# Input projection of a hybrid mixer block: three-pass product on 128-token slabs replaced by Strassen's scheme on 2x2x2 blocks, tokens in two halves

## Chip, cores and metric

One core of a Trainium2 chip. The metric is the device time of one execution in microseconds (us); lower is better. The profile is one execution taken by the hardware profiler on that core. Engines: TensorE (PE for its matmuls, PEld for its weight loads), VectorE (DVE), ScalarE (ACT), GpSimd (POOL) and SyncE (SP, here only an issuer of DMAs).

## What is computed

A pre-norm block on 2048 tokens of width 1024, all float32:

```python
u = rms_norm(h, norm_in_g)
proj = einsum('bsd,de->bse', u, w_in)          # 2048 x 1024 times 1024 x 4096
pool_x, pool_z, m_x, m_z = split(proj, 4)      # 1024 columns each
y_pool = pool_mixer(pool_x, pool_w, pool_scale) * silu(pool_z)   # window means, then pool_w
y_m = mlstm_branch(m_x, ...) * silu(m_z)       # conv, headwise q/k/v, two scans over 16 chunks
h = h + einsum('bse,ed->bsd', concatenate([y_pool, y_m]), w_out)
return rms_norm(h, norm_out_g)
```

Float32 products are made of float32r matmuls: each operand is split into a high part and the rest, and high x high, high x low and low x high are added in PSUM.

## The kernel before

The projection is worked in 32 column slabs of 128 columns by 4 token blocks of 512 tokens. `project` (L135) makes one block of one slab: 8 steps over the 1024 inputs, 3 matmuls each, 24 matmuls of 128x128 by 128x512 into one PSUM tile `proj`; 128 blocks give 3072 matmuls. The normalising factor is not in the operand: x is multiplied by the norm's gain and split as it lands (`uh` by ACT on L217, `ul` by DVE on L218), the factor per token (`rnorm`, L226 to L248) is multiplied in when DVE empties the PSUM tile (L204, L408, L543, L550). A weight slab is loaded whole (`wl`, 512 KB), its high part cast by ACT (L91), its rest made by DVE (L94); it serves all four token blocks. The split of x stays in SBUF for the whole projection.

The order of the slabs: the eight mLSTM slabs first (the *m phase*), then four slabs of m_z, sixteen for the pooling branch (two per pooling slab: `ux` and `sz`), then the other four of m_z. In the m phase each block's columns go through a convolution over tokens (DVE, L314 and L316, five operations of 512 columns, then ACT's silu on L318), and `headwise` (L336 to L346): products to q-k and v maps per 128 tokens, copied out of PSUM by ACT as `tokst` (L337), transposed (L344), copied again as `kkTb` (L346), stored; `gacc` (POOL, L339) sums the gates' rows. In the same phase `fold` multiplies pool_w into the pool_x columns of w_in: 32 steps, each of 6 small matmuls (L185) into a PSUM tile `hw` that `headwise` uses too (3 buffers), a copy by ACT to one tile `st` (L188) and a store to the scratch tensor `wp_s` that ACT's own queue issues (L189). `st` has one buffer, so a copy waits until the store before it has landed. The pooling slabs load their weights from `wp_s`.

After the m phase the gates of all tokens are turned into the scan's tables (L420 to L520): a long chain of small DVE operations with a few matmuls (L456 to L517), beside the first m_z slabs. The last m_z slabs are interleaved with the first steps of the backward scan (`next_backward`, L597). Then comes the main loop, the rest of both scans with the output product (L685), which the change does not touch apart from how it is started.

A scheduler lists the instructions of each engine in an order that respects the data and the buffers and goes by its own estimate of times; from `ordered.append(True)` on the matmuls keep the order in which they are written.

## Time and profile before

| | us |
|---|---|
| median of 3 runs | 1522.79 (1521.84 to 1523.7) |
| profiled execution, its own time | 1520.88 |
| span of that execution, first to last instruction | 1519.2 |
| PE busy / DVE busy / ACT busy / POOL busy | 1493.2 / 845.6 / 494.6 / 359.8 |
| mean granted TensorE clock | 0.994 of full |
| DMA moved | 231 MB, 152 GB/s |

The profiled execution lies 1.7 us above its span and 1.9 us below the median. The projection's last matmul (L135) starts at 858.8 us, the rest of the span is the main loop. [...]

### The profile page before, as it was taken

The page shows a single profiled execution, that of the slowest core. Times are in us where ns is not written, and L with a number is a line of the kernel's source. Part 1 is how long each engine was busy: PE and PEld are TensorE (multiplying, and loading weights), DVE is VectorE, ACT ScalarE, POOL GpSimd, SP SyncE. Part 2 cuts the span into 40 slices and gives each one's busy share as a digit, 9 for nine tenths or more (in the row PEclk, how much of TensorE's full clock was granted, in tenths as well). Part 3 has the DMA queues.
Part 4 walks back from the last instruction along what each step waited for, and adds up shares of the span by engine and source line. Part 5 has one row for each costly group of instructions (what it writes and reads, how often), then busy time and mean ns, then how long its engine had stood idle before and what let it go on. Part 6 is the DMA issues. An engine that isn't in the chain of part 4 may idle for free.

```text
span 1519.2 us, 21070 instructions
## 1 busy us (share of the span) xinstructions
PE 1493.2 (98%) x7193; PEld 1259.9 (83%) x7193; DVE 845.6 (56%) x1700; ACT 494.6 (33%) x1144; POOL 359.8 (24%) x549
## 2 busy tenths in 40 slices
PE   8899999999999999999999999999999999999998
PEld 6788888878888888888888878888888888888886
DVE  8896355563133333445433377767777777665553
ACT  6344433343110011011112444444344445433331
POOL 5544333310000210222200123233332323121100
PEclk8999999999999999999999999999999999999999
DMA  6268765552201111111053787877777778765442
GB/s 223 66 201 234 211 181 169 167 164 80 77 14 56 56 44 53 56 56 44 26 159 107 225 245 233 234 228 207 224 223 216 222 211 262 200 194 156 139 135 84
DMA packets 251339, 231.11 MB, mean 152 GB/s; under 512 B 18400, under 2 KB 211168, under 8 KB 250208
## 3 DMA queue, kind: packets, MB, share of 16 engines
q1 hardware_dynamic: 236768, 215.08, 47.9%
q10 hardware_dynamic: 14464, 14.68, 3.0%
q8 instruction: 57, 0.93, 0.3%
q14 instruction: 50, 0.41, 0.1%
HBM read 149.81 MB, written 79.89 MB: 151 GB/s over the span
## 4 chain that ended last, share of the span: by engine, by line
PE 91%; DVE 3%; DMA 3%; ACT 1%; POOL 1%; issue 1%; SPq 0%; DVEq 0%; POOLq 0%; ACTq 0%
PE proj L135 42%; PE po L685 23%; PE upd L597 7%; PE num L817 7%; PE hw L336 4%; PE num L812 4%; PE sT L802 2%; PE hw L185 1%; PE py L869 1%; DVE ul L218 1%; PE hw L344 1%; DVE c L316 1%; DMA kk<-kk_s 1%; DMA xt<-in_xT 1%; DMA wost<-in_w_out 1%
## 5 line engine op out<-in xcount | busy, mean ns | idle before, releaser
L135 PE MATMUL proj<-uh,whi 128*128 128x512 f32 x1024 | 407.7, 398 | 3.7 <-DVE mx L204 2.3
L135 PE MATMUL proj<-ul,whi 128*128 128x512 f32 x1024 | 402.3, 393 | 2.1 <-DVE ul L218 2.1
L135 PE MATMUL proj<-uh,wlo 128*128 128x512 f32 x1024 | 402.5, 393 | 0.0
L135 PEld LDWEIGHTS proj<-uh,whi 128*128 128x128 f32 x1024 | 194.4, 190 | 43.1 <-DVE mx L204 2.4
L135 PEld LDWEIGHTS proj<-ul,whi 128*128 128x128 f32 x1024 | 194.1, 190 | 41.8 <-DVE ul L218 2.4
L135 PEld LDWEIGHTS proj<-uh,wlo 128*128 128x128 f32 x1024 | 193.9, 189 | 41.2
L685 PE MATMUL po<-woh,yh 128*128 128x512 f32 x512 | 217.6, 425 | 0.0
L685 PE MATMUL po<-woh,yl 128*128 128x512 f32 x512 | 201.5, 394 | 0.0
L685 PE MATMUL po<-wol,yh 128*128 128x512 f32 x512 | 201.3, 393 | 0.0
L597 PE MATMUL upd<-v,kw 128*128 128x258 f32 x480 | 124.2, 381 | 3.1 <-ACT hh L833 1.9
L791 POOL TENSOR_TENSOR cw<-cT,gw 128x512 f32<-128x512 f32 (+1 forms) x64 | 79.0, 1234 | 168.5 <-issue 77.9
L685 PEld LDWEIGHTS po<-woh,yl 128*128 128x128 f32 x512 | 96.2, 188 | 22.1
L685 PEld LDWEIGHTS po<-wol,yh 128*128 128x128 f32 x512 | 96.6, 189 | 19.2
L685 PEld LDWEIGHTS po<-woh,yh 128*128 128x128 f32 x512 | 96.4, 188 | 19.1
L91 ACT CAST whi<-wl 128x1024 fp32r<-128x1024 f32 x31 | 32.6, 1052 | 229.0 <-PE proj L135 225.9
L316 DVE SCALAR_TENSOR_TENSOR c<-mx,par_sb,c 128x512 f32<-128x512 f32 x128 | 103.6, 827 | 3.0
L597 PEld LDWEIGHTS upd<-v,kw 128*128 128x128 f32 x480 | 87.3, 190 | 14.9 <-ACT hh L833 2.0
L543 DVE TENSOR_TENSOR ux<-proj,rnorm 128x512 f32<-128x512 f32 x32 | 22.1, 692 | 124.7 <-PE proj L135 124.7
L784 POOL TENSOR_SCALAR_AFFINE_SELECT gw<-gw 128x128 f32<-128x128 f32 x128 | 43.8, 365 | 172.6 <-DMA gw<-g_s 170.5
L875 ACT ACTIVATE yt<-cT,par_sb 128x128 f32<-128x128 f32 x128 | 44.5, 394 | 108.8 <-DMA ym_s<-yt 108.7
L851 POOL TENSOR_TENSOR rstd<-rstd,mhalf 128x1 f32<-128x1 f32 x64 | 35.1, 549 | 174.5 <-DVE rstd L849 99.8
L833 ACT ACTIVATE hh<-num,rn 128x256 f32<-128x256 f32 x64 | 30.1, 471 | 141.9 <-DVE rn L829 133.8
(194 smaller groups left out, 2184.5 us busy)
## 6 DMA issues: line engine op xcount, KB each, us to landing
gw<-g_s SPq DMA_DIRECT2D x128, 128.0 KB, 4.8
v<-v_s SPq DMA_DIRECT2D x124, 129.0 KB, 4.5
kk<-kk_s SPq DMA_DIRECT2D x124, 128.0 KB, 4.0
wl<-in_w_in SPq DMA_DIRECT2D x23, 512.0 KB, 3.8
xt<-in_xT SPq DMA_DIRECT2D x32, 256.0 KB, 4.8
cT_s<-c SPq DMA_DIRECT2D x32, 256.0 KB, 3.7
kk_s<-tokst SPq DMA_DIRECT2D x32, 256.0 KB, 2.5
kkT_s<-kkTb SPq DMA_DIRECT2D x32, 256.0 KB, 4.1
```

Of the source, the lines that this page charges most:

```text
L91: nc.scalar.copy(hi, src)
L135: pe(nc.tensor.matmul(ps, lhsT=l[:, kt, :], rhs=r[:, kt, :], start=(kt == 0 and n == 0), stop=(kt == KT - 1 and n == 2)))
L316: nc.vector.scalar_tensor_tensor(c, in0=mx[:, b * BT + t:(b + 1) * BT + t], scalar=par_sb[:, i, t:t + 1], in1=c, op0=ALU.mult, op1=ALU.add)
L336: nc.tensor.matmul(ps[:, e, :], lhsT=src[:, o:o + P], rhs=rhs, start=True, stop=True)
L597: pe(nc.tensor.matmul(ps[:, m, :E], lhsT=t["kw"][:, ms], rhs=t["v"], start=True, stop=True))
L685: pe(nc.tensor.matmul(ps, lhsT=l[:, kt, :], rhs=r, start=(kt == 0 and e == 0), stop=(kt == 7 and e == 2)))
L784: nc.gpsimd.affine_select(out=a["gw"][:, 0, d, :], in_=a["gw"][:, 0, d, :], compare_op=ALU.is_ge, fill=BIG, base=0, pattern=[[pat, P]], ch ...
L791: eng.tensor_tensor(a["cw"][:, ds], a["cT"][:, None].broadcast_to([P, nd, 2, P]), a["gw"][:, 1, ds, None, :].broadcast_to([P, nd, 2, P]), ...
L812: pe(nc.tensor.matmul(num[:, d, :E], lhsT=a["dd"][:, d, :], rhs=a["kv"]["v"], start=True, stop=d not in a["dirs"]))
L817: pe(nc.tensor.matmul(num[:, d, :E], lhsT=a["cw"][:, d, m, :], rhs=state[:, m, :], start=False, stop=(m == 1)))
L851: nc.gpsimd.tensor_tensor(a["rstd"][:, 0:1], a["rstd"][:, 0:1], mhalf[:, :1], op=ALU.pow)
L875: nc.scalar.activation(a["yt"][:, m, :], a["cT"][:, m, :], AF.Copy, scale=par_sb[:, i, 8:9])
```

## The change

**Halves.** Tokens are worked in two halves of 1024. In each half all 16 *units* are done in the order m0 to m3, z0, p0 to p7, z1 to z3; a unit is two column slabs of 128 (for p: one of `wp_s` and its z) by two token blocks of 512.

**Seven products.** Each unit takes seven products of 4 input steps x 3 matmuls = 12 matmuls (L153), in the order P1, P5, P6, P2, P7, P3, P4, against 96 matmuls for the same outputs before: 2 x 16 x 84 = 2688 matmuls. P1, P5 and P6 are partial sums: ACT copies them out of PSUM (`snap`, L160), the accumulation in the PSUM tile goes on. P2, P7 and P3 are emptied by DVE as PSUM plus such a copy, P4 by ACT or straight by silu. PSUM: `psy` two tiles, `psx` and `psz` one each.

**Operands.** The weight operands of a unit are 7 quarter sets of 128 x 512, 4 of them sums or differences made by POOL (L141), each cast by ACT (L97) and its rest made by DVE (L100); this is done in both halves, so weights are loaded and prepared twice. The x operands (B) are 7 sets per half; they need the normalised x, so x is scaled in place by gain and factor first (16 DVE operations, L219), then 16 differences (8 on DVE, 8 on POOL, L231) and 28 casts (ACT) and 28 rests (DVE) of 512 columns. The sets of P1 and P2 need the first token block alone, the other five need both. Half 1's x is loaded, scaled and prepared during units 13 to 15 of half 0.

**m phase.** Convolution and `headwise` go in chunks of 4 and 3 token groups (half 0) and 3 x 3 (half 1), and the map tables and a halo of x's tail are passed through DRAM (`mv_s`, `mt_s`). All 32 fold steps are asked for one or two per product from the first unit on, with the fold's tiles in single buffers. The gates' tables come after half 1's m phase, in a pool of their own that is closed before the pooling units' pool is opened at the same addresses.

**End.** Units 13 to 15 of half 1 stand in the written order with `next_backward` after each product; in the last one the main loop's first loads are issued as the x operands' pools close (`room`).

```diff
+    def prepare_a(u, k):
+        w1, w2 = raw[u, 0], raw[u, 1]
+        a11, a12, a21, a22 = w1[:, :4], w1[:, 4:], w2[:, :4], w2[:, 4:]
+        if k in ("P5", "P6", "P7", "P3"):
...
+            v = sums[k] = ap.tile([P, 4, P], F32, name="sum", bufs=3)
+            nc.gpsimd.tensor_tensor(v, x, y, op=op_)
...
+        split(v, hi, lo, nc.vector)
+        A[u, k] = (hi, lo)
+
+    def product(u, k, ps, first):
+        (ah, al), (bh, bl) = A.pop((u, k)), B[k]
+        for q in range(4):
+            for n, (l, r) in enumerate(((ah, bh), (ah, bl), (al, bh))):
+                pe(nc.tensor.matmul(ps, lhsT=l[:, q, :], rhs=r[:, q, :], start=(first and q == 0 and n == 0),
+                                    stop=(q == 3 and n == 2), skip_group_check=not first))
...
+    def unit(u, nxt, put, between):
+        for n, k in enumerate(PRODUCTS):
+            if k == "P1":
+                y = banks["y"] = psp.tile([P, BT], F32, name="psy", bufs=2)
+            bank = "x" if k == "P2" else "z" if k in ("P5", "P3") else "y"
+            if k in ("P5", "P2"):
+                banks[bank] = psp.tile([P, BT], F32, name=f"ps{bank}")
+            ps = banks[bank]
+            product(u, k, ps, k in ("P1", "P5", "P2"))
+            if k in ("P1", "P5", "P6"):
+                snap(k, ps)
+            elif k == "P4":
+                put(1, 0, ps, None)
+            else:
+                e, t, other = {"P2": (0, 0, "P1"), "P7": (1, 1, "P5"), "P3": (0, 1, "P6")}[k]
+                put(e, t, ps, snaps[other])
+            if nxt:
+                prepare_a(nxt, k)
+            between(n)
...
+    def scale_x(t, kt):
+        nc.vector.scalar_tensor_tensor(xs[t, kt], in0=xs[t, kt], scalar=par_sb[:, kt, 9:10], in1=rn[t], op0=ALU.mult,
+                                       op1=ALU.mult)
...
+    def prepare_b(k):
+        hi = bpool[k].tile([P, 4, BT], F32R, name=f"bh{k}")
+        lo = bpool[k].tile([P, 4, BT], F32R, name=f"bl{k}")
+        for q in range(4):
+            x11, x12, x21, x22 = xs[0, q], xs[1, q], xs[0, 4 + q], xs[1, 4 + q]
+            v = {"P1": x11, "P5": x11, "P6": x11, "P2": x21, "P7": x12, "P3": x22, "P4": x21}[k]
+            if k in ("P5", "P6", "P7", "P4"):
+                x, y = {"P5": (x12, x11), "P6": (x22, x11), "P7": (x22, x12), "P4": (x21, x11)}[k]
+                (nc.vector if k in ("P5", "P6") else nc.gpsimd).tensor_tensor(v, x, y, op=ALU.subtract)
+            split(v, hi[:, q], lo[:, q], nc.vector)
+        B[k] = (hi, lo)
+
+    plan = [("m", i) for i in range(4)] + [("z", 0)] + [("p", i) for i in range(8)] + [("z", i) for i in range(1, 4)]
...
+    folds = (None for g in range(4) for _ in fold(g))
+    for p in range(2):
...
+        if p == 0:
+            fop = open_pool(pm, "fop", bufs=1)
+        for n in range(5):
+            u = plan[n]
+
+            def between(k, n=n):
+                chunk_step(p)
+                if p == 0:
+                    next(folds, None)
+                    if n:
+                        next(folds, None)
...
+        if p:
+            pmp.close()
+            with ExitStack() as pz:
+                gp = open_pool(pz, "gp")
+                psg = open_pool(pz, "psq", bufs=2, space=PSUM)
+                gate_rows()
+        with ExitStack() as pz:
+            zp = open_pool(pz, "pp", bufs=2)
+            for n in range(5, 13):
+                put, ux, sz = put_p(p, plan[n])
+                unit(plan[n], after(p, n), put, lambda k: None)
...
+                for n in range(13, 16):
+                    unit(plan[n], after(p, n), put_z(p, plan[n]), lambda k, n=n: between(k, n))
```

The order of three places, before and after. ACT in the m phase, among the fold's copies and stores; `c` is the convolution's silu, `mv` and `mw` the map tables, `P_` a copied partial sum, `tokst` and `kkTb` headwise's results. Before:

```order
L188 COPY st<-hw 128x256
L189 DMA wp_s<-st 128x2x128
L188 COPY st<-hw 128x256
L189 DMA wp_s<-st 128x2x128
L188 COPY st<-hw 128x256
L189 DMA wp_s<-st 128x2x128
L318 ACTIVATE c<-c,par_sb 128x512
L305 COPY mw<-pg 128x16
L306 ACTIVATE mw<-pg 128x128
L307 COPY vw<-pg 128x16
L337 COPY tokst<-hw 128x2x144 x4
L346 COPY kkTb<-hw 128x512
```

After:

```order
L269 COPY st<-hw 128x256
L270 DMA wp_s<-st 128x2x128
L269 COPY st<-hw 128x256
L270 DMA wp_s<-st 128x2x128
L321 ACT_TABLE_LOAD
L321 ACTIVATE c<-c,par_sb 128x512
L321 ACTIVATE c<-c,par_sb 128x384
L296 COPY mv<-pg 128x16
L297 ACTIVATE mv<-pg 128x128
L298 COPY mv<-pg 128x16
L160 COPY P_774<-psz 128x512
L269 COPY st<-hw 128x256
```

Before, 32 copies stand in 179 rows of ACT; after, they stand in 155 rows, and 169 projection matmuls stand among the folds' on PE.

PE where the gates' tables end (`decr`, `mpr`, `glr`, `gm`, `wsr` are the tables; `pg` its PSUM tile). Before:

```order
L135 MATMUL proj<-uh_113,wlo 128x512
L499 MATMUL pg<-decr,ones 128x128
L500 MATMUL pg<-ones,mpr 128x1
L501 MATMUL pg<-ones,glr 128x1
L135 MATMUL proj<-uh_113,whi 128x512
L135 MATMUL proj<-ul_114,whi 128x512
L135 MATMUL proj<-uh_113,wlo 128x512
L135 MATMUL proj<-uh_113,whi 128x512
L135 MATMUL proj<-ul_114,whi 128x512
L516 MATMUL pg<-ident,gm 128x128
L135 MATMUL proj<-uh_113,wlo 128x512
L135 MATMUL proj<-uh_113,whi 128x512
```

After:

```order
L153 MATMUL psy<-bhP_4091,alP_6138 128x512
L551 MATMUL pg<-decr,ones 128x128
L552 MATMUL pg<-ones,mpr 128x1
L553 MATMUL pg<-ones,glr 128x1
L568 MATMUL pg<-ident,gm 128x128
L569 MATMUL pg<-ident,wsr 128x128
L153 MATMUL psx<-bhP_4191,ahP_6196 128x512
L153 MATMUL psx<-blP_4192,ahP_6196 128x512
L153 MATMUL psx<-bhP_4191,alP_6197 128x512
L153 MATMUL psy<-bhP_4288,ahP_5879 128x512
```

Before, projection matmuls stand between the first three and each of the last two; after, the five stand in a row, ahead of the next unit's `psx` and of the fourth product of the unit before (`psy`).

DVE at the same place after (`ux` and `sz` are the pooling unit's results):

```order
L560 TENSOR_SCALAR gm<-g_6034,mg 128x128
L570 TENSOR_TENSOR em_tok<-pg,b_tok 128x128
L572 COPY ws_tok<-pg 128x128
L407 TENSOR_TENSOR ux<-psx,P_6135 128x512
L411 TENSOR_TENSOR sz<-psy,P_6154 128x512
L407 TENSOR_TENSOR ux<-psz,P_6174 128x512
```

The three results of the pooling unit, two of which PE's next tiles wait for, stand behind the last row of the gates' chain.

DVE at the start. Before (`ul` is the rest of x's split, `sq` a square's sum, `mx` an emptied PSUM tile):

```order
L218 SCALAR_TENSOR_TENSOR ul_114<-xt,par_sb,uh_113 128x512 x4
L230 TENSOR_TENSOR sq<-sq 128x512
L228 TENSOR_TENSOR sq<-sq 128x512 x2
L230 TENSOR_TENSOR sq<-sq 128x512
L218 SCALAR_TENSOR_TENSOR ul_109<-xt,par_sb,uh_108 128x512
L230 TENSOR_TENSOR sq<-sq 128x512
L218 SCALAR_TENSOR_TENSOR ul_109<-xt,par_sb,uh_108 128x512
L204 TENSOR_TENSOR mx<-proj,rnorm 128x512 x2
L218 SCALAR_TENSOR_TENSOR ul_109<-xt,par_sb,uh_108 128x512 x5
```

After, from the second token block's scaling on (`x_` a block of x, `bl` a rest of an x operand, `bh` its cast):

```order
L219 SCALAR_TENSOR_TENSOR x_182<-x_182,par_sb,rn_314 128x512
L219 SCALAR_TENSOR_TENSOR x_184<-x_184,par_sb,rn_314 128x512
L231 TENSOR_TENSOR x_150<-x_170,x_150 128x512
L231 TENSOR_TENSOR x_152<-x_172,x_152 128x512
L231 TENSOR_TENSOR x_154<-x_174,x_154 128x512
L100 TENSOR_TENSOR blP_325<-x_150,bhP_324 128x512
L100 TENSOR_TENSOR blP_325<-x_152,bhP_324 128x512
L100 TENSOR_TENSOR blP_325<-x_154,bhP_324 128x512
L231 TENSOR_TENSOR x_156<-x_176,x_156 128x512
```

Before, a rest needs the cast of the same block alone; after, a block is scaled by the norm's result, then differences are taken, and the rests come from these.

## Rows read from the trace of the kernel before

**Rows 1.** The page: chain that ended last, shares by engine and line.

```profile
PE 91%; DVE 3%; DMA 3%; ACT 1%; POOL 1%; issue 1%; SPq 0%; DVEq 0%; POOLq 0%; ACTq 0%
PE proj L135 42%; PE po L685 23%; PE upd L597 7%; PE num L817 7%; PE hw L336 4%; PE num L812 4%; PE sT L802 2%; PE hw L185 1%; PE py L869 1%; DVE ul L218 1%; PE hw L344 1%; DVE c L316 1%; DMA kk<-kk_s 1%; DMA xt<-in_xT 1%; DMA wost<-in_w_out 1%
```

**Rows 2.** Windows (us): sum, busy by engine (instructions), clock, DMA share, GB/s.

```profile
0.00:80.00 80.00, 68.88 (x302) 56.69 (x303) 65.26 (x74) 36.32 (x60) 46.52 (x45) 0.89 0.45 145
...
100.00:320.00 220.00, 216.38 (x1325) 193.18 (x1324) 119.38 (x158) 98.75 (x232) 81.15 (x168) 1.00 0.70 196
```

**Rows 3.** Windows of the projection's line alone: sum, PE, PEld busy.

```profile
0.00:80.00 80.00, 57.94 (x210) 44.10 (x211) 0.89 0.45 145
...
100.00:320.00 220.00, 125.27 (x509) 92.93 (x509) 1.00 0.70 196
...
340.00:764.00 424.00, 423.22 (x1865) 349.40 (x1863) 1.00 0.15 53
```

**Rows 4.** Windows of the start, columns as in the second group.

```profile
0.00:20.00 20.00, 15.42 (x58) 12.86 (x59) 13.95 (x14) 13.03 (x19) 9.94 (x17) 0.83 0.82 286
...
40.00:60.00 20.00, 15.16 (x66) 12.28 (x65) 20.00 (x20) 7.92 (x13) 15.04 (x11) 0.90 0.37 107
```

**Rows 5.** Groups by form: line, engine, tiles, count, busy us, mean ns, idle before.

```profile
L218 DVE SCALAR_TENSOR_TENSOR ul<-xt,par_sb,uh 128x512 fp32r<-128x512 f32 x32 | 35.3, 1152 | 0.0
...
L204 DVE TENSOR_TENSOR mx<-proj,rnorm 128x512 f32<-128x512 f32 x32 | 21.7, 687 | 85.9 <-PE proj L135 82.7 <-ACT rnorm L248 3.1
...
L94 DVE TENSOR_TENSOR wol<-wost,woh 128x512 fp32r<-128x512 f32 x9 | 6.1, 690 | 5.5 <-ACT woh L91 3.3 <-DMA sz_s<-op 2.2
...
L217 ACT ACTIVATE uh<-xt,par_sb 128x512 fp32r<-128x512 f32 x32 | 21.0, 711 | 1.3 <-DMA xt<-in_xT 1.3
...
L188 ACT COPY st<-hw 128x256 f32<-128x256 f32 x32 | 11.8, 368 | 37.3 <-DMA wp_s<-st 32.0 <-PE hw L185 3.3 <-PE pg L304 1.7
```

**Rows 6.** Timeline of DVE at the start: start, us, operation, count.

```profile
53.15 5.33 DVE L218 SCALAR_TENSOR_TENSOR ul<-xt,par_sb,uh 128x512 fp32r<-128x512 f32 x4
...
59.60 2.06 DVE L218 SCALAR_TENSOR_TENSOR ul<-xt,par_sb,uh 128x512 fp32r<-128x512 f32 x3
```

**Rows 7.** Timeline of POOL at the start, same columns.

```profile
46.25 1.47 POOL L240 TENSOR_TENSOR rs<-rs,mhalf 128x4 f32<-128x4 f32 x1 [1.36 <-DVE rs L239]
...
52.75 1.37 POOL L226 TENSOR_TENSOR sq<-xt 128x512 f32<-128x512 f32 x1
54.09 1.73 POOL L228 TENSOR_TENSOR sq<-sq 128x512 f32<-128x512 f32 x1
```

**Rows 8.** The fold's tile: copies, what ACT waited for (us, times), landing.

```profile
L188 ACT COPY st<-hw x32: 349/372/387, 87.9 to 311.9; 128x256 f32<-128x256 f32 x32
...
  DMA wp_s<-st: 32.0, 9
...
DMA to landing us min/median/max: 1.8/3.2/4.9
```

**Rows 9.** Timeline of ACT at three fold copies in a row.

```profile
226.19 0.37 ACT L188 COPY st<-hw 128x256 f32<-128x256 f32 x1 [4.21 <-DMA wp_s<-st]
...
228.48 0.37 ACT L188 COPY st<-hw 128x256 f32<-128x256 f32 x1 [1.92 <-DMA wp_s<-st]
```

**Rows 10.** Timeline of DVE along the gates' chain.

```profile
323.61 0.23 DVE L424 COPY fx<-gacc 128x128 f32<-128x128 f32 x1 [2.48 <-POOL gacc L339]
...
350.66 0.29 DVE L502 COPY dec_bc<-pg 128x128 f32<-128x128 f32 x1 [0.67 <-PE pg L501]
...
355.23 0.28 DVE L520 COPY ws_tok<-pg 128x128 f32<-128x128 f32 x1
```

**Rows 11.** Timelines of two weight rests, alone and beside POOL.

```profile
454.72 1.23 DVE L94 TENSOR_TENSOR wlo<-wl,whi 128x1024 fp32r<-128x1024 f32 x1 [0.17 <-ACT whi L91]
...
476.39 3.62 POOL L556 TENSOR_TENSOR win<-ux 128x2063 f32<-128x2063 f32 x1 [17.92 <-DVE ux L543]
476.52 4.58 DVE L94 TENSOR_TENSOR wlo<-wl,whi 128x1024 fp32r<-128x1024 f32 x1 [0.21 <-ACT whi L91]
```

More of the change, by code (lines that the diff above doesn't have):

```diff
@@ new lines, in product, with snap @@
+    def product(u, k, ps, first):
[4 more added lines that the diff above has]
+                                    stop=(q == 3 and n == 2), skip_group_check=not first))
+    banks, snaps = {}, {}
+    def snap(name, ps):
+        snaps[name] = ap.tile([P, BT], F32, name=name)
+        nc.scalar.copy(snaps[name], ps)
@@ new lines, in hymba_block, with chunk_step, put_mx, put @@
+    CHUNKS = (((0, 4), (4 * P, 3)), tuple((FIRST + 3 * n * P, 3) for n in range(3)))
+    convs, maps = [], []
+    def chunk_step(p):
+        if maps:
+            headwise(p, *maps.pop(0))
+        if convs:
+            maps.append(convs[0])
+            conv(p, *convs.pop(0))
+    def put_mx(p, u):
+        def put(e, t, ps, other):
+            i = 2 * u[1] + e
+            if i not in made:
+                new_mx(p, i)
+                made.add(i)
+            a = at(p, p * S // 2 + t * BT)
+            dst = mxs[i][:, a:a + BT]
+            if other is None:
+                nc.scalar.copy(dst, ps)
+            else:
+                nc.vector.tensor_tensor(dst, ps, other, op=ALU.add)
+            if p == 0 and t == 1:
+                nc.sync.dma_start(out=mt_s[i], in_=mxs[i][:, FIRST:])
+        made = set()
+        return put
@@ L395, in hymba_block @@
-    phw.close()
-    def z_slab(zp, i, order):
-        w = load_w(w_in[24 + i])
-        for b in order:
-            z_block(zp, i, w, b)
-    def z_block(zp, i, w, b, between=None):
-        ps = project(w, b, range(KT // 2))
-        if between:
-            between()
-        project(w, b, range(KT // 2, KT), ps)
-        sz = zp.tile([P, BT], F32, name="op")
-        nc.vector.tensor_tensor(sz, ps, rnorm[:, b * BT:(b + 1) * BT], op=ALU.mult)
-        nc.scalar.activation(sz, sz, AF.Silu)
-        nc.scalar.dma_start(out=sz_s[i][:, b * BT:(b + 1) * BT], in_=sz)
```

573 lines of the change are left out of this document (278 added, 295 removed).

## Prediction

> **What bounds the kernel now.** I read the chain of waits first: TensorE holds 91% of it, and 42% of the span is the projection's line alone [rows 1]. So matmuls taken out of the projection are worth their full time wherever TensorE is never late. The windows tell where that is. From 340 to 764 us it is busy all the time, and the projection's line has 1865 matmuls in 423.2 us [rows 3], 0.227 us each. In the first 80 us it is busy 68.9, and VectorE 65.3 [rows 2]; from 40 to 60 VectorE is never idle and TensorE is at 15.2 of 20 [rows 4]. From 100 to 320 TensorE is busy 216.4 of 220 [rows 2]. So two kinds of stretch: those where fewer matmuls are time gained, and the start and the m phase, where the other engines are close behind. I read next what the change puts on these. The main loop after 859 us is not touched.
>
> **The gain.** 3072 - 2688 = 384 matmuls x 0.227 = **-87 us**. A product is 12 x 0.227 = 2.72 us, a unit 19.05. In the pooling and z units I expect this in full: a unit asks VectorE for 7 weight rests (0.69 each [rows 5]) and 3 evacuations (0.69), 7 us, a pooling unit's windows on 1032 columns for up to four operations at twice 0.69, 6 more, within 19; the copies of partial sums lie two products ahead of their use. These costs I set at nothing; TensorE's work covers them. Elsewhere:
>
> **Start.** Before, TensorE has 210 projection matmuls done by 80 us [rows 3], because a block of x is split as it lands. After, only P1 and P2 can start on the first norm, the rest wait for the second. GpSimd carries the norms: per block 4 squares of 1.37, 2 sums of 1.73 and a power of 1.47 [rows 7], 10.4 us, plus 3 weight sums before the first power; from the first landing at about 6 us that gives the first norm at 6 + 10.4 + 3 x 1.4 + some 5 of waits, about 26. VectorE then scales 8 blocks, makes 8 rests and the square sums (20 operations), and the second norm comes out near 49 (20 x 0.69, 8 of them slowed beside GpSimd by 0.6, and some 4 for the power and its spreading). The price of that neighbour: four rests in a row took 5.33 us beside GpSimd and three took 2.06 alone [rows 6], 1.33 against 0.69. Then 8 scalings, 8 differences and 20 rests stand on VectorE: 36 x 0.69 = 25, and 10 slowed by 0.6 make 31, to 80; the last product ends near 82. By then TensorE has about 99 matmuls of the projection. 111 missing x 0.227 = 25, and 2 us past 80: **+28** (21 to 35, the ends being all pairs alone and all slowed).
>
> **Folds.** This is the largest unknown. The order puts all 32 fold copies into 155 rows of ScalarE, while TensorE's matching rows hold 169 projection matmuls (38.3 us) and 192 fold, 56 headwise (two records each), 28 transposes and 15 map matmuls. In 100 to 320 the small ones cost (216.4 - 509 x 0.227) / (1325 - 509) = 0.124 per record [rows 2, 3], so 347 x 0.124 = 43 and TensorE has 81 us to do there. ScalarE's own operations in those rows sum to 59 us (32 copies at 0.37, 17 casts, 36 headwise copies and so on, by their groups as in [rows 5]). But each copy waits for the store of the copy before it: one buffer, and the store is issued behind it on the same queue. Before, nine such waits took 32.0 us, 3.6 each; the landing is 1.8 to 4.9, median 3.2 [rows 8], and a copy right behind another waited 4.21 and 1.92 [rows 9]. Going through the 155 rows with one landing time for all, ScalarE needs 81 us at 1.9, 98 at 2.5, 104 at 2.7, 116 at 3.1, 129 at 3.55 and 158 at 4.5. Queued behind the waiting copy are the copies of partial sums, the weight casts and headwise's copies, so TensorE waits too. Before, the copies were spread over 225 us and their waits of 32 us hidden. The stores carry the same bytes beside similar traffic, so I take 3.1, next to the median: 115 - 81 = **+33** (0 to 50).
>
> **Half 1's x.** During units 13 to 15 VectorE gets 16 scalings, 8 differences, 28 rests, 14 weight rests and 6 evacuations with the norm's sums: about 76 x 0.7 = 53 us, and some 22 beside GpSimd's differences and sums pay 0.6 each, together 66. It can start when the first norm is there, about 24 us into unit 13 (load of 4 MB at the 286 GB/s of the first 20 us [rows 4], 15 us, and the norm). 24 + 66 + 2.7 = 93, where TensorE would be through with half 1's first unit at 4 x 19.05 = 76: **+17** (8 to 28).
>
> **Gates.** The chain from the summed gates to the table of decays took 323.6 to 350.7, 27 us, and to the last table 355.2 [rows 10]. Before, TensorE had z slabs to do beside it, without end. After, the next pooling unit's results wait, in VectorE's order and for their addresses, behind the chain; the PSUM tiles fill, and the matmuls in TensorE's order ahead of L551 are some 18 us. So 27 - 18 = 9, then 5 from the decays to the last table with nothing between, and about 3 until three evacuations (0.69 each [rows 5]) free PSUM: **+17** (12 to 22). The cover that is gone is the z slabs.
>
> **Rest.** Half 1's m phase: per unit TensorE has 19 and 18 token groups x 5 records x 0.124 = 11, together 30, and VectorE 10 operations of 0.69 and 6 convolutions of five operations on 384 columns (16), together 23: hidden but for single waits, +2 (0 to 8). The start of the main loop, whose first loads are now issued some 5 us later against the last product: +4 (0 to 10). No row shows either; the bounds are one evacuation more or less per product and one landing of 4.9 us [rows 8] twice. What TensorE lost before in 80 to 859 us (about 5 us, of it 3.6 in 100 to 320 [rows 2]) is contained in these terms: -5.
>
> **Sum.** -87 + 28 + 33 + 17 + 17 + 2 + 4 - 5 = +9. The profiled execution was 1520.9, so 1530. It lies 1.9 under the median of the runs, within their spread of 2.
>
> **Rivals.**
>
> *The folds hide.* If the stores land in about 1.9 us the stretch falls to TensorE's 81 and the term to nothing: 1530 - 33 = **1497**, faster than before. For it: the least landing is 1.8, and one of two waits in a row was 1.92 [rows 9]; in half 0 fewer stores of headwise run beside. Against it: nine waits at 3.6 on average. It decides below a landing of about 2.7 us: there the stretch is 104, and the whole sum is near nothing.
>
> [...] One weight rest of 1.23 us took 4.58 when GpSimd's addition of 3.62 began just before it [rows 11], close to the sum of both, 4.85. If every pair at the start and in half 1's preparation paid the plain sum, the 10 and 22 pairs would each pay GpSimd's 1.4 instead of 0.6, +8 and +18: about **1556**. Against it: a pair of short operations took 1.33 + 1.37 side by side, not one after the other [rows 6, 7]. [...]
>
> [...]
>
> *The change doesn't do what it says:* the products could come out slower than 0.227 where `psx` and `psz` have one tile each; an evacuation of 0.69 against a product of 2.72 between speaks against it.
>
> **Chances.** Forecast 0.53 (own range 1512 to 1548), folds hidden 0.25, port 0.14, clock 0.08. Faster and slower by more than 0.2% (3 us) is about what a measurement of this kernel can tell from no change. Faster: folds hidden 0.25 and the forecast's lower end 0.06, 0.31. Within 0.2% of 1522.8: 0.10, from the forecast's middle of small landings. Slower: 0.59. The range runs from folds hidden with the gates at their lower bound, 1494, to the port's 1560; left out are the clock and a tail of the port and of the folds, 0.15.
>
> **What would show it.** The changed kernel's product line has 2688 matmuls; in a pooling unit 84 of them take 19 us. The first unit's last matmul stands near 80 us, with VectorE full from 50. Between 82 and 200 us ScalarE's copies wait for stores, 50 to 60 us in all, and TensorE's idle time there is ended by ScalarE. TensorE waits for VectorE's rests of x operands at the turn of the halves (near 470 to 490), and for the gates' chain once, 15 us or more, ahead of L551. The last matmul of the projection starts near 868. It is wrong if the waits for stores are short and TensorE is full in the fold stretch, or if the preparation of x takes no longer than TensorE's units beside it.

## The result and the profile after

The changed kernel takes 1635.55 us (median of 4 runs, 1634.38 to 1636.11) against 1522.6 for the kernel before in the same comparison: ratio 1.074 (95% interval 1.0722 to 1.0759), 113 us slower. The prediction was 1530, with a range to 1560. The profiled run has a span of 1632.7, 113.5 above the span before.

From the page of the changed kernel come the busy line of TensorE and the others (busy us, share, instructions), the granted clock in 40 slices, and the chain that ended last by engine (to be set against [rows 1]).

```profile
PE 1470.6 (90%) x6809; PEld 1210.9 (74%) x6809; DVE 1021.5 (63%) x1994; ACT 650.4 (40%) x1506; POOL 579.7 (36%) x763
...
PEclk6699999999988999979999989999999999999999
...
PE 58%; DVE 9%; DMA 9%; issue 5%; POOL 4%; ACT 3%; SPq 0%; POOLq 0%; DVEq 0%; ACTq 0%
```

TensorE's share of the last chain fell from 91% to 58%. It is busy 1470.6 us, 22.6 less than before, though 384 matmuls of 0.227 were taken out, 87 us: some 64 us were given back, most of it by matmuls at a lower granted clock (slices 1, 2, 12, 13, 18 and 24 of the clock row, at 0.6 to 0.8 of full, show it best; the mean granted clock is 0.954, against 0.994). The rest of the loss is idle time, 162 us of the span against 26.

Next the windows of the changed kernel, cut at the ends of its units (the 84th, 168th, ... matmul of the product line); columns as in [rows 2].

```profile
0.00:86.80 86.80, 43.74 (x139) 31.31 (x140) 65.57 (x80) 32.38 (x55) 47.27 (x42) 0.63 0.24 79
86.80:275.80 189.00, 160.03 (x857) 128.69 (x856) 86.87 (x122) 80.26 (x202) 86.02 (x150) 0.96 0.62 178
275.80:333.00 57.20, 57.20 (x254) 47.37 (x253) 29.15 (x34) 20.86 (x37) 25.49 (x23) 1.00 0.25 84
333.00:457.00 124.00, 116.01 (x505) 94.09 (x504) 71.62 (x82) 43.29 (x75) 68.88 (x55) 1.00 0.28 96
457.00:516.70 59.70, 48.49 (x201) 39.30 (x199) 51.67 (x60) 26.12 (x47) 31.86 (x22) 0.89 0.27 91
516.70:691.50 174.80, 152.71 (x767) 126.87 (x767) 132.68 (x197) 91.09 (x217) 56.92 (x100) 0.94 0.49 154
691.50:753.50 62.00, 48.47 (x204) 38.68 (x203) 40.99 (x133) 20.22 (x39) 19.84 (x43) 0.86 0.28 91
753.50:875.00 121.50, 115.78 (x505) 94.20 (x504) 70.37 (x82) 41.65 (x72) 63.85 (x51) 1.00 0.23 79
875.00:955.60 80.60, 73.44 (x313) 59.93 (x311) 35.19 (x50) 29.79 (x55) 14.38 (x12) 0.96 0.41 129
955.60:1632.70 677.10, 654.73 (x3077) 550.45 (x3076) 437.35 (x1156) 264.72 (x714) 165.20 (x271) 0.99 0.69 201
```

And the product line alone in three of them, as in [rows 3]:

```profile
0.00:86.80 86.80, 33.78 (x85) 21.64 (x86) 0.63 0.24 79
86.80:275.80 189.00, 95.25 (x337) 61.60 (x336) 0.96 0.62 178
...
516.70:691.50 174.80, 114.85 (x421) 82.31 (x420) 0.94 0.49 154
```

Taking a product matmul at 0.227 and a small record at 0.124 (both worked out from [rows 2, 3]), each stage can be set against the TensorE work that is in it:

| stage (us of the changed kernel) | length | TensorE's work at full clock | loss | predicted |
|---|---|---|---|---|
| start, to the first unit's end (0 to 86.8) | 86.8 | 125 product matmuls fewer than before at 80, and 6.8 later | 35 | 28 |
| half 0, units 1 to 4 with the folds (86.8 to 275.8) | 189.0 | 337 x 0.227 + 520 x 0.124 = 141 | 48 | 33 |
| pooling and z units (275.8 to 457 and 753.5 to 875) | 302.7 | 1264 x 0.227 = 287 | 16 | 0 |
| turn of the halves (457 to 516.7) | 59.7 | 169 x 0.227 and 32 of one column = 40 | 20 | 17 |
| half 1, units 0 to 4 (516.7 to 691.5) | 174.8 | 421 x 0.227 + 346 x 0.124 = 138 | 36 | 2 |
| gates, units 5 and 6 (691.5 to 753.5) | 62.0 | 42 | 20 | 17 |
| last units (875 to 955.6) and the main loop behind them | 80.6 and 677.1 | 70, and 660.2 as before | 10 and 17 | 4 |

The losses sum to 202; less the 87 of the change's gain and the 5 that TensorE lost before, 110 of the 113.5 are found. In the pooling and z units TensorE runs at full clock and a unit takes 19.0 to 20.9 us, so the gain itself is there.

**Where it waits.** Each place is shown by lines of the timelines (start, us, engine, operation, idle time before and what ended it). First a pooling unit, GpSimd, then ScalarE, then TensorE:

```profile
341.60 1.29 POOL L141 TENSOR_TENSOR sum<-w 128x512 f32<-128x512 f32 x1 [2.57 <-DMA w<-in_w_in]
...
344.28 0.62 ACT L97 CAST ahP<-sum 128x512 fp32r<-128x512 f32 x1 [0.74 <-POOL sum L141]
344.80 0.58 ACT L160 COPY P<-psy 128x512 f32<-128x512 f32 x1
...
345.43 0.50 PE L153 MATMUL psy<-bhP,ahP 128*128 128x512 f32 x1 [1.45 <-ACT P L160]
```

The weight load has one buffer per tile and was issued at 337.7, when the unit before had read it. GpSimd's sum waits for it, ScalarE's cast waits for the sums, and behind that cast in ScalarE's queue stands the copy of a partial sum which frees TensorE's tile: 1.45 us here. Eleven of the fifteen pooling and z units of the table take 20.1 to 20.9 us in place of 19.0. Over the whole run such waits for a weight load come to 123.5 us of GpSimd and ScalarE.

Next half 1's m phase, the same three engines:

```profile
590.71 1.27 POOL L141 TENSOR_TENSOR sum<-w 128x512 f32<-128x512 f32 x1 [5.08 <-DMA cT_s<-c]
...
592.02 0.62 ACT L97 CAST ahP<-sum 128x512 fp32r<-128x512 f32 x1 [3.02 <-POOL sum L141]
...
593.02 1.29 ACT L341 COPY tokst<-hw 128x288 f32<-128x288 f32 x4
...
598.80 0.61 ACT L321 ACTIVATE c<-c,par_sb 128x384 f32<-128x384 f32 x1 [3.97 <-DVE c L319]
...
600.31 1.28 ACT L341 COPY tokst<-hw 128x288 f32<-128x288 f32 x4
...
593.48 0.51 PE L340 MATMUL hw<-mv,mx 128*128 128x144 f32 x2 [1.78 <-ACT tokst L341]
...
600.76 0.51 PE L340 MATMUL hw<-mv,mx 128*128 128x144 f32 x2 [2.25 <-ACT tokst L341]
```

At 590.71 GpSimd's sum starts after 5.08 us; its weights were asked for at 586.3, behind five stores in SyncE's queue (the wait is put down to a store that came with it). ScalarE's cast waits for the sum, headwise's copies stand behind the cast, and TensorE waits 1.78 for them; five us later the head of ScalarE's queue is a silu that waits 3.97 for VectorE's convolution, and TensorE waits 2.25 for the copies behind it. That convolution had itself begun late, behind a rest that waited 2.95 us for ScalarE's cast, so the two waits hang together. The windows right there show the clock around such a gap:

```profile
599.00:603.00 4.00, 2.24 (x11) 1.91 (x12) 2.59 (x5) 2.95 (x8) 0.59 (x2) 0.90 0.41 130
603.00:607.00 4.00, 4.00 (x20) 3.51 (x19) 2.11 (x5) 2.00 (x5) 0.27 (x1) 0.68 0.32 116
```

In 603 to 607 TensorE is busy all the time and granted 0.68 of full clock (0.50 from 603 to 605, then 0.70 and 1.00 in a microsecond each): behind the gap it loses time again. The same is seen at the start, where a matmul ahead of a wait of 5.05 us took 0.39 and the one behind it 0.79; from 60 to 80 us the granted clock was 0.50:

```profile
53.71 0.39 PE L153 MATMUL psy<-bhP,alP 128*128 128x512 f32 x1
59.15 0.79 PE L153 MATMUL psz<-bhP,ahP 128*128 128x512 f32 x1 [5.05 <-ACT bhP L97]
```

Not every gap is paid so: the pooling units of 333 to 457 us have 8 us of idle time in gaps like the one above, and a clock of 1.00.

Then the turn of the halves, and the gates, both on TensorE (the last line is from the table of waits between 691.5 and 753.5: us in total, times, longest):

```profile
463.12 1.86 PE L207 MATMUL pg<-ones,sq 128*128 128x1 f32 x8 [4.14 <-DVE sq L203]
...
478.26 1.02 PE L207 MATMUL pg<-ones,sq 128*128 128x1 f32 x8 [3.91 <-DVE sq L203]
```

```profile
709.60 0.66 PE L508 MATMUL pg<-lfr,le 128*128 128x64 f32 x2 [4.70 <-DVE lfr L500]
...
727.90 0.79 PE L551 MATMUL pg<-decr,ones 1*128 1x128 f32 x2 [6.34 <-ACT decr L549]
...
PE psx L153 <- DVE ux L407: 1.2, 1, 1.2
```

In both, small matmuls of a norm or of the gates' chain stand early in TensorE's order and it waits in line for VectorE's sums (8.1 us), the table's transposed rows (4.7) and the decays (6.3). For a pooling unit's result it waited 1.2 us in the gates' two units. Last, the start of the main loop (SyncE, ScalarE, TensorE):

```profile
969.58 0.38 SPq L736 DMA_DIRECT2D y<-yp_s  x1
...
977.54 0.40 ACT L97 CAST yh<-y 128x256 fp32r<-128x256 f32 x1 [11.33 <-DMA y<-yp_s]
...
978.00 0.79 PE L759 MATMUL po<-woh,yh 128*128 128x512 f32 x1 [7.80 <-ACT yh L97]
```

The second y is asked for at 969.6, lands at 977.5, and TensorE stands for 7.8 us.

### The profile page after: what moved, and what is told of

Same layout as the page of the kernel before. It is cut to its first block, busy times and chain, and to the rows that moved or that the text cites. A ratio compares the mean times of both kernels' runs of the same rounds, so it can differ in the third digit from the quotient of the medians.

```text
span 1632.7 us, 21715 instructions
## 1 busy us (share of the span) xinstructions
PE 1470.6 (90%) x6809; PEld 1210.9 (74%) x6809; DVE 1021.5 (63%) x1994; ACT 650.4 (40%) x1506; POOL 579.7 (36%) x763
## 4 chain that ended last, share of the span: by engine, by line
PE 58%; DVE 9%; DMA 9%; issue 5%; POOL 4%; ACT 3%; SPq 0%; POOLq 0%; DVEq 0%; ACTq 0%
PE po L759 20%; PE psy L153 10%; PE upd L672 6%; PE num L891 6%; PE psz L153 5%; PE num L886 3%; PE psx L153 2%; DVE alP L100 2%; POOL win L430 2%; PE hw L340 2%; POOL sum L141 2%; PE sT L876 2%; DVE c L319 1%; DMA w<-in_w_in 1%; DMA wost<-in_w_out 1%
## 5 line engine op out<-in xcount | busy, mean ns | idle before, releaser
L153 PE MATMUL psy<-bhP,ahP 128*128 128x512 f32 x512 | 214.2, 418 | 25.3 <-ACT P L160 18.0
L153 PE MATMUL psy<-blP,ahP 128*128 128x512 f32 x512 | 209.5, 409 | 4.4 <-DVE blP L100 4.4
L153 PE MATMUL psy<-bhP,alP 128*128 128x512 f32 x512 | 207.8, 406 | 0.0
L100 DVE TENSOR_TENSOR alP<-sum,ahP 128x512 fp32r<-128x512 f32 x128 | 122.3, 956 | 104.6 <-ACT ahP L97 94.3
L97 ACT CAST ahP<-sum 128x512 fp32r<-128x512 f32 x128 | 79.2, 620 | 206.3 <-POOL sum L141 96.6
L153 PEld LDWEIGHTS psy<-bhP,ahP 128*128 128x128 f32 x512 | 101.6, 199 | 52.6 <-ACT P L160 24.2
L153 PEld LDWEIGHTS psy<-blP,ahP 128*128 128x128 f32 x512 | 101.3, 198 | 26.2 <-DVE blP L100 6.6
L153 PEld LDWEIGHTS psy<-bhP,alP 128*128 128x128 f32 x512 | 100.9, 197 | 20.7
L319 DVE SCALAR_TENSOR_TENSOR c<-mx,par_sb,c 128x384 f32<-128x384 f32 (+1 forms) x160 | 113.8, 719 | 3.9
L153 PE MATMUL psz<-bhP,ahP 128*128 128x512 f32 x256 | 103.6, 405 | 6.7 <-ACT bhP L97 6.1
L153 PE MATMUL psz<-blP,ahP 128*128 128x512 f32 x256 | 102.0, 398 | 1.7 <-DVE blP L100 1.7
L97 ACT CAST ahP<-w 128x512 fp32r<-128x512 f32 x96 | 59.4, 620 | 110.5 <-PE psy L153 70.2
L153 PE MATMUL psz<-bhP,alP 128*128 128x512 f32 x256 | 101.7, 397 | 0.0
```

Of the source, the lines that this page charges most:

```text
L97: nc.scalar.copy(hi, src)
L100: lo_eng.tensor_tensor(lo, src, hi.bitcast(F32), op=ALU.subtract)
L153: pe(nc.tensor.matmul(ps, lhsT=l[:, q, :], rhs=r[:, q, :], start=(first and q == 0 and n == 0), stop=(q == 3 and n == 2), skip_group_check ...
L319: nc.vector.scalar_tensor_tensor(c[:, :m], in0=mx[:, o + t:o + t + m], scalar=par_sb[:, i, t:t + 1], in1=c[:, :m], op0=ALU.mult, op1=ALU.add)
```

## The experiments

Times are medians; ratios are to the kernel before in the same comparison, with 95% intervals. The changed kernel itself is at 1.074. A difference of 0.003 is 4.6 us. Stages are read from one profiled execution of each kernel, and a stage that an edit doesn't touch differs between kernels too: half 0's units 1 to 4 took 186.6 to 193.3 us in the changed kernel and the five whose edits lie elsewhere, half 1's units 0 to 4 took 173.2 to 176.8 in seven such, and units 5 and 6 of half 1 took 60.4 to 63.6 in eight.

**The store behind the fold's copy.** `a_st3`:

```diff
-            st = fop.tile([P, 2, P], F32, name="st", bufs=1)
+            st = fop.tile([P, 2, P], F32, name="st", bufs=3)
```

> The changed kernel with three buffers in place of one for the fold's copied tile, so that a copy need not wait for the store before it. Theory A (the prediction's fold term: landings of the stores hold ScalarE, and TensorE behind it): the time falls by about 33 us, 1600, and the loss of half 0's m phase (86.8 to 275.8 us, 189 us against 141 us of TensorE work) mostly goes. Theory B (in-order queues: ScalarE's copies out of PSUM stand behind whatever its head waits for, and the store is only one of several such heads; the trace shows 15.2 us of waits for stores and TensorE held 6.9 us by these copies): the time falls by 5 to 12 us, 1624 to 1631.

It takes 1633.27 us, ratio 1.0721 (1.069 to 1.0752): 2 to 3 us less, and the interval holds the changed kernel's 1.074. What ScalarE waited for in front of the copies and their landings, first in the changed kernel, then here:

```profile
  DMA wp_s<-st: 15.2, 11
...
DMA to landing us min/median/max: 1.8/2.4/6.6
```

```profile
  PE hw L266: 32.6, 24
  DMA wp_s<-st: 4.2, 2
```

The prediction's largest cost is not there: 15.2 us of waits in all, landings of 2.4, and when those waits go, the copies wait for the folds' matmuls instead (32.6 us), with TensorE hardly earlier: units 1 to 4 took 186.8 us, within what untouched kernels show. Theory B's 5 to 12 us aren't there either.

**The folds as a whole**, left out of both kernels. `a_nofold` and `b_nofold` (lines of the first's edit):

```diff
-        for e, t in enumerate((wp_s[i], w_in[8 + i]) ...
+        for e, t in enumerate((w_in[i], w_in[8 + i]) ...
...
-                    next(folds, None)
```

> The changed kernel without the folds (the 32 steps that multiply pool_w into the weights are left out; the pooling units take their unfolded weights from the input). TensorE's share of the folds is 192 matmuls x 0.12 = 23 us. Theory A (the folds and their single buffers make half 0's loss): falls by 23 + 40 or more, to 1570 or less. Theory B (headwise's copies behind casts and silus in ScalarE's queue make it, folds or not; half 1, which has no folds, loses 36 us as well): falls by 23 + 10 to 20, 1593 to 1603.

> The kernel before without the folds, left out in the same way; it gives the folds' price there. Both theories: TensorE is busy throughout that phase, so its 23 us of fold matmuls go and little else, 1497 to 1502.

The changed kernel without folds takes 1595.01, 1.047 (1.0439 to 1.05), 41 us less; the kernel before takes 1497.96, 0.9833 (0.9803 to 0.9863), 25.5 less, TensorE's own work of 23 and little more. So the folds cost 15 us more in the changed kernel than before. The four units without folds:

```profile
86.80:237.00 150.20, 126.65 (x665) 107.28 (x664) 84.04 (x122) 69.29 (x169) 36.70 (x70) 0.95 0.58 163
```

They take 150.2 us for 337 x 0.227 + 328 x 0.124 = 117 us of work: two thirds of half 0's loss is there without any fold.

**The fold's split weights.** `a_fop2`: two buffers for `wh` and `wlf` (`bufs=1` to `bufs=2` in the pool).

> The changed kernel with two buffers for the fold's split weights (wh, wlf), as the kernel before has. Leaving the folds out took 40.5 us from the changed kernel and 25.6 from the one before; three buffers for the copied tile took 2. Theory D (the other 13 us are TensorE waiting in line for GpSimd's split of the next weights, 11.4 us in the trace, because one buffer lets it begin only after the fold before): 8 to 13 us less, 1622 to 1627. Rival (the folds cost through ScalarE's and PSUM's queues): under 4 us.

It takes 1629.06, 1.0708 (1.0666 to 1.075), 5 to 6 us less with an interval that holds 1.074. Units 1 to 4 took 186.1 in place of 189.0, next to the lowest of the untouched kernels. The theory's 8 are not shown, nor is a smaller share of the 15 for these buffers or for the store. TensorE's wait for GpSimd's split of these weights, 11.4 us in the changed kernel and none in the kernel before, is still there with two buffers, 11.9; it is the largest wait that comes with the folds, and what holds the split back was not tried.

**Weight loads.** `a_w2`: a second pair of raw weight tiles for every other unit, where SBUF has room:

```diff
-            raw[u, e] = ap.tile([P, KT, P], F32, name=f"w{e}")
+            raw[u, e] = (wide[0] or ap).tile([P, KT, P], F32, name=f"w{e}")
...
+            w2 = open_pool(pz, "w2p")
```

> The changed kernel with a second pair of raw weight tiles, used by every other unit in half 1's m phase and in both halves' pooling units, so that the next load need not wait until the unit before has read its weights. Theory B (a late weight load holds GpSimd's sums, these ScalarE's casts, and behind the casts stand the copies of partial sums that TensorE waits for: 20.5 us per pooling unit in place of 19.0, and gaps in half 1's m phase): every second pooling unit comes to 19.0 us, and half 1's m phase gains some; together 12 to 25 us less, 1611 to 1624. [...]

It takes 1621.8, 1.0625 (1.0583 to 1.0666), 14 to 17 less. Six pooling and z units of half 0 (8 to 13) now:

```profile
338.00:452.00 114.00, 114.00 (x504) 94.41 (x503) 62.46 (x82) 41.82 (x73) 56.95 (x50) 1.00 0.26 86
```

They take 114.0 us in place of 124.0, TensorE busy throughout, 19.0 per unit where they took 20.4 to 20.9, and half 1's units 7 to 12 take 19.0 each as well. The chain from the load to the partial sum's copy is the whole loss of these units. Half 1's m phase gained 4 (170.9 us). These stages gain 21 together; the turn of the halves took 4 longer (63.9), so the whole run shows less.

**The gates.** `a_gate` keeps the tables' pool open beside the pooling units' (both in one `with`); `a_gatesplit` does that and cuts the chain in four parts that are written behind units 4, 5, 7 and 8:

```diff
+        yield
         pr = psg.tile([P, 512], F32, name="pg")
         nc.tensor.matmul(pr[:, :P], lhsT=ones[:1, :], rhs=flat(decr), start=True, stop=True)
...
+                if p and n in (5, 7, 8):
+                    next(gates, None)
```

> The changed kernel with the gates' tables in a pool that stays open beside the first pooling units of half 1, so that their results have addresses of their own and the scheduler may put them between the rows of the gates' chain. The prediction's gate term (results and PSUM behind the chain): 12 to 22 us go, 1613 to 1623, and units 5 and 6 of half 1 take 40 to 45 us together in place of 62. Rival (VectorE's chain itself and its place in the queue hold TensorE, whatever the addresses): under 5 us.

> The changed kernel with the gates' tables in a pool that stays open (as in a_gate, which gained 1 us) and, in addition, the chain written in four parts, behind units 4, 5, 7 and 8 of half 1, so that the chain's matmuls stand later in TensorE's order: 150 product matmuls (34 us) now lie between the table's transposed rows and the decays, where it was 83 rows or fewer. Theory C (addresses don't matter; TensorE's order reaches the chain's matmuls before VectorE has their operands and waits in line): units 5 and 6 of half 1 take 38 to 43 us in place of 62, total 15 to 22 us less, 1613 to 1621. Rival (VectorE's chain takes the results' place in its own queue whatever the matmuls' order): under 6 us.

`a_gate` takes 1634.52, 1.0729 (1.0698 to 1.076), 1 to 2 less, which can't be told from nothing. Units 5 and 6 of half 1:

```profile
699.10:756.60 57.50, 48.00 (x203) 38.30 (x203) 44.20 (x132) 23.99 (x42) 19.67 (x43) 0.91 0.25 78
```

They took 57.5 in place of 62.0, some 3 to 6 us below the untouched kernels; TensorE's two waits for the chain are still there, 4.4 us each. `a_gatesplit` takes 1621.67, 1.0659 (1.0628 to 1.069), 12 to 14 less, and for the same units:

```profile
691.80:742.10 50.30, 43.67 (x195) 34.84 (x194) 41.93 (x127) 19.49 (x34) 20.09 (x43) 0.97 0.28 87
```

They take 50.3 us, clock 0.97 where it was 0.86, short of the theory's 38 to 43. Of TensorE's waits for the chain's operands one of 1.2 us is left; ahead of two `psy` tiles it now waits 3.0 and 2.4 us for VectorE. So the addresses held TensorE for the smaller part, and the chain's place in the order for the larger. The edit moves the chain's rows on VectorE and ScalarE together with its matmuls, and was not tried without the open pool; these were not parted.

**The convolution.** `a_noconv`: the four multiply-adds of a chunk are left out.

```diff
-        for t in range(1, 5):
+        for t in range(0):
```

> The changed kernel with the convolution cut to its first operation (the four multiply-adds per chunk are left out), so that VectorE is hardly asked in the m phase. Theory B (ScalarE's silu waits for VectorE's convolution, 46 us in half 1, and headwise's copies wait behind it): half 1's five m-phase units fall from 174.8 us to about 150, half 0's gain 5 to 15: 1595 to 1608. Rival (headwise's own buffers, two of its result tile and three of its PSUM tile, hold TensorE): under 10 us in all.

It takes 1611.24, 1.0556 (1.0519 to 1.0592), 24 to 28 less. Half 1's five units:

```profile
511.90:669.30 157.40, 146.63 (x767) 123.82 (x767) 68.79 (x102) 90.22 (x219) 52.31 (x100) 0.97 0.59 172
```

They take 157.4 in place of 174.8 (about 150 was expected), with the same work on TensorE and on ScalarE. VectorE's convolution, 64 us of work there on an engine that is busy 133 of 175, cost 17 us. What ScalarE's silu waited for in the stage, in total, first in the changed kernel, then here:

```profile
ACT c L321 <- DVE c L319: 46.1, 23, 4.0
...
ACT c L321 <- DVE c L317: 4.6, 5, 1.1
```

TensorE's wait for headwise's copies behind it fell from 15.0 us to 2.4. ScalarE's casts also waited less for GpSimd's sums (3.6 us in place of 12.5), so the silu is the larger part of the path but not shown to be all of it.

**Headwise's own tiles.** `a_tok`: `tokst` with four buffers and `c` with five in half 1.

> The changed kernel with four buffers for headwise's result tile and five for the convolution's chunk in half 1 (two and three before). Rival of the convolution in ScalarE's queue (leaving it out took 18 us from half 1's m phase): headwise waits for its own tiles' stores; GpSimd waited 30.6 us for them in half 1. If so 10 to 20 us less. Theory B (in-order heads other than these tiles): under 5 us.

It takes 1634.74, 1.0707 (1.0679 to 1.0734); its span is 1633.0 against 1632.7: nothing that can be told from zero in the whole run. The stage itself:

```profile
519.90:689.70 169.80, 147.13 (x767) 123.93 (x767) 129.92 (x196) 90.61 (x217) 62.03 (x106) 0.97 0.54 160
```

It took 169.8 in place of 174.8, below the untouched kernels, while half 0's units 1 to 4 took 191.2. GpSimd's waits for these tiles' stores fell from 30.6 us to 3.8. TensorE's idle time stayed at 22 to 23 us, and the gain stands in its clock, 0.97 in place of 0.94. So these long waits cost 5 us of the stage at most.

**Gaps and clock.** `a_fill`: six unused matmuls of 512 columns behind each product of half 1's m phase.

```diff
+                if p:
+                    f = psg.tile([P, 512], F32, name="pg")
+                    for _ in range(6):
+                        nc.tensor.matmul(f, lhsT=B["P1"][0][:, 0, :P], rhs=B["P1"][0][:, 0, :], start=True, stop=True)
```

> The changed kernel with six more matmuls of 512 columns behind each of the 35 products of half 1's m phase (210 in all, 47.6 us of TensorE at 0.227; their results are not used). Theory E (that phase's 36 us of loss are gaps and the matmuls at the lower clock behind them, which more work in line fills): the phase gets longer by 12 to 25 us and its granted clock rises from 0.94 to 0.99 or more; total 1648 to 1660. Rival (TensorE's own rows are the length of the phase and each added matmul comes on top): 40 to 48 us longer, 1676 to 1683, clock about as before.

It takes 1654.89, 1.0878 (1.0831 to 1.0924), 19 to 21 more for 47.6 us of added work. The phase:

```profile
515.00:711.50 196.50, 189.23 (x971) 159.69 (x970) 126.34 (x197) 94.15 (x218) 55.51 (x104) 0.99 0.46 139
```

It takes 196.5 in place of 174.8, clock 0.99 in place of 0.94. TensorE is idle 7.3 us there in place of 22.1, and its busy time grew by 36.5. So 26 of the 48 us came without length: 15 went into gaps, and 11 came from matmuls that had run at the lower clock.

**The norm and scaling of x.** `a_plainx`: both left out, the operands are made of x as it lands.

> The changed kernel without the norm of x and its scaling (left out in both halves; the operands are made of x as it lands). Prediction's steps (the norms and 16 scalings stand ahead of the operands): the first unit ends near 55 us in place of 86.8, and the turn of the halves (units 13 to 15 and the first of half 1) gains 10 to 17: 1590 to 1595. Rival (the 28 rests and casts alone set the start): the first unit ends above 70 us, gain under 20 in all.

It takes 1593.91, 1.0442 (1.0398 to 1.0486), 42 to 45 less. The start and units 14 and 15 of half 0:

```profile
0.00:57.50 57.50, 33.17 (x118) 25.69 (x118) 49.89 (x56) 27.44 (x51) 30.74 (x31) 0.76 0.41 141
427.90:475.90 48.00, 41.88 (x169) 33.16 (x167) 30.87 (x33) 22.32 (x41) 18.96 (x12) 0.93 0.34 111
```

The first unit ends at 57.5 (86.8), the two units take 48.0 (59.7). The two terms were placed rightly; at the turn the wait was the norm's matmuls in TensorE's order, not the rests of the operands, of which TensorE waited 0.6 us in half 1.

**The loads of the main loop.** Three kernels from the one before. `b_late` and `b_late2` write the opening of the pools and their loads one block later, or all behind the last; `b_late3` works the last pair's blocks in the order 3, 1, 0, 2, so that the addresses come free late.

```diff
-        for b in range(NB):
+        for b in (range(NB) if pair != (6, 7) else (3, 1, 0, 2)):
```

> The kernel before, with the main loop's first loads (output weights, first y, first steps) each issued one token block, about 11 us, later against the projection's last matmul, as the change does through its operands' pools. If the 17 us that the changed kernel loses after its last projection matmul come from these late loads: 6 to 15 us slower than before, 1528 to 1537, with TensorE idle in the 40 us after the projection. Rival (they come from the backward scan's first steps or the clock after the gaps): within 3 us of before.

> The kernel before with all first loads of the main loop issued behind the last token block, none before it (one block late cost 1.7 us). The changed kernel issues them within its last 14 us. Theory F (the 17 us after its last projection matmul are these loads, which come too late): 8 to 25 us slower than before, 1532 to 1548. Rival (the loop's start waits for something else in the changed kernel, its backward scan's first steps or DMA traffic): under 5 us.

> The kernel before with the last pair of slabs worked in the token order 3, 1, 0, 2, so that the main loop's output weights (whose addresses are those of block 0's operands) can be loaded only behind the third block, 11 us ahead of the end, and the first steps' tiles behind the last. The two kernels that only moved the loads in the text issued them at the same times as before, since they wait for the addresses. Theory F (the changed kernel's 17 us behind its last projection matmul are loads that can't start until its last unit frees the operands' addresses): 8 to 25 us slower than before, with TensorE idle right after the projection. Rival: under 4 us.

`b_late` takes 1526.77, 1.0011 (1.0 to 1.0022), `b_late2` 1522.33, 1.0002 (0.9991 to 1.0013). Both say nothing on the question: the loads were issued at the same times (the first y at 827.6 and 826.8, at 826.6 before), which fits loads that wait for the address and not for their place in the text. `b_late3` takes 1540.02, 1.0086 (1.006 to 1.0112), 13 us slower. The window behind its projection, the load of its first step on SyncE, and TensorE's first wait:

```profile
862.00:900.00 38.00, 24.05 (x91) 19.16 (x92) 13.68 (x31) 14.10 (x31) 6.38 (x13) 0.78 0.82 239
...
863.50 0.51 SPq L769 DMA_DIRECT2D cT<-cT_s  x1
...
868.83 1.20 PE L802 MATMUL sT<-cT,kkT 128*128 128x128 f32 x4 [7.20 <-DMA cT<-cT_s]
```

TensorE is busy 24 of 38 us there, clock 0.78, where the kernel before has 37.9 of 41 at full clock in 859 to 900. So loads that must wait for the last operands' addresses, with the new order of the blocks, cost 13 us (9 to 17 by the interval), close to the 17 of the changed kernel. It is the same kind of delay and not the same load: here TensorE's longest wait is for the first step's `cT`, asked for 2 us behind the last projection matmul, and the two y were asked for 10 ahead of it and 19 behind. In the changed kernel `cT` was asked for 8 us ahead and the long wait is for the second y. In it the first y was asked for at 942.2, 13 us ahead of the last projection matmul, and the second at 969.6, 14 us behind it; in the kernel before they were at 826.6 and 840.8, 32 and 18 us ahead.

**Three mends together.** `a_all`: `a_gatesplit`, `a_w2` and `a_fop2` in one.

> The changed kernel with three mends together: the gates' chain in four parts, the second pair of raw weight tiles, two buffers for the fold's split weights. Singly 13.9, 13.8 and 6.5 us less. They act at different places, so theory C with B and D: 30 to 36 us less, 1600 to 1606, still slower than the kernel before. Rival (they feed the same later wait): under 24 us less.

It takes 1605.89, 1.0519 (1.0495 to 1.0543): 30 to 34 us less than the changed kernel, about the sum of the three (34). They don't feed one common wait. It is still 80 us slower than the kernel before; no kernel made from the changed one is faster than that.

## Why the prediction was wrong

**The gain** of 87 us was right: 19.0 us per unit wherever nothing waits (`a_w2`).

**Start, turn and gates** (28, 17, 17) came out at 35, 20 and 20. For the first the mechanism holds: the norms' factors reach TensorE at 25.6 and 50.6 us (26 and 49 were worked out), and `a_plainx` takes 29 us away; the size was 7 short. For the turn it was the norm and scaling, as said, but not the wait that was named: TensorE waited 0.6 us for rests of x operands, and 8.1 in line for the norm's sums. That the number came close is luck. For the gates the step failed in its mechanism: it was said that results and PSUM tiles queue behind the chain; TensorE waited 1.2 us for a result and 11.9 for the chain's own operands. With addresses of their own the two units gained 3 to 6 us, and with the chain later in the order 12 to 14 us came back in all.

**Folds** (33, from landings of 3.1 us): the stage lost 48, but the term's step failed altogether. The landings were 2.4, the waits 15.2 where 50 to 60 were expected, and taking them away gave 2 us, which is no more than the scatter. The price of the folds beyond before's is 15, and no run here locates it; the rest of the stage's loss is the m phase's own, as in half 1. (By the term's own list a landing of 3.1 gives 116 us and not 115, so 35; and the range's lower end, folds hidden and gates at their lower bound, adds up to 1492 and not 1494. Neither matters beside 113.)

**Half 1's m phase** (2) is the step that failed most: 36. The prediction set two busy sums per unit side by side, 30 of TensorE and 23 of VectorE, took the smaller one as hidden, and left ScalarE's queue out. VectorE's sum was in fact 27 and ScalarE's 18, both still the smaller. What counts is the order in ScalarE's queue: copies that free PSUM for TensorE stand behind casts that wait for GpSimd's sums and behind silus that wait for VectorE. `a_noconv` gives 17 of it, `a_w2` 4, `a_tok` 5 at most; if these add up, the other 10 were not taken apart.

**Pooling units** (0): 16. The copies of partial sums may lie "two products ahead of their use", but they stand in one queue with casts that wait for a load: `a_w2` takes all of it.

**End** (4): 27. The loads were said to be 5 us later against the last product; the first y was 19 later and the second 32, and `b_late3`, which delays them in a like way, prices such a delay at 13. The 10 us in the last units begin with a gap of 6.1 us, for which the profile names no releaser; in it GpSimd's sum waits 5.7 us for a weight load again. It was not tried apart.

**Clock.** A lower clock was given 0.08 and left out of the range. It was no single event: it came with many of the gaps, and by the mean granted clocks (1470.6 x 0.046 less 1493.2 x 0.006, an estimate) some 59 of the 64 us that TensorE's busy time gave back are its work. It is a part of the losses above and not a cause beside them: `a_fill` and `a_gatesplit` raise the clock where they fill or close gaps (0.94 to 0.99 and 0.86 to 0.97).

The forecast's other error is in its form: seven terms with ranges were added as if they were independent, and the terms set near nothing for the m phase and the pooling units had the same hidden assumption, that a queue's head doesn't wait.

## What to carry to other kernels

When a change gives an engine's queue more kinds of work, don't compare busy sums (ScalarE's 18 us per unit were the smaller, and headwise's copies behind a cast that waited 3.02 us made TensorE wait 1.78): list, for each instruction that frees what TensorE needs next, what stands ahead of it in its queue and what that waits for, down to the load. A scheduler's order is fixed by its own estimates; small matmuls of a long chain that stand early in TensorE's order make it wait in line (4.7 and 6.3 us for the gates' chain), and can be moved by writing the chain's parts later. A saving in TensorE's work is only worth its time where TensorE is the one that is late, and a gap can be followed by a second loss, in clock, as two of the gaps above show (0.68 from 603 to 607 us, 0.50 from 60 to 80).

## What the runs showed of the hardware that was not expected

In `a_gate` four of VectorE's smallest operations took 1.14 to 1.21 us, nearly as long as the GpSimd operation beside them (1.27 to 1.30). The first of them, VectorE, then GpSimd:

```profile
737.34 1.21 DVE L543 TENSOR_TENSOR mrow<-glr,rows 1x8 f32<-1x8 f32 x1
...
737.24 1.29 POOL L141 TENSOR_TENSOR sum<-w 128x512 f32<-128x512 f32 x1 [0.91 <-DMA w<-in_w_in]
```

An operation on 8 elements that takes 0.15 elsewhere took 1.21 and ended at 738.55; GpSimd's sum of 1.29 had begun 0.10 earlier and ended at 738.53. VectorE's operation took 1.06 us longer beside the sum, where the forecast allowed 0.6 us per pair and the rival of 1556 ("port" in the chances) GpSimd's 1.4. In the changed kernel's own trace the same operation never took more than 0.16, where GpSimd did nothing beside it; but 128 weight rests of VectorE took 0.956 on average there, against 0.69 alone. How many of them met a GpSimd operation, and how much of the 113 us this makes, was not tried.
